# Scaling the rows before a transpose at the turns of blocks, in a two-layer diffusion trunk on one core

## Chip, cores and metric

The kernel runs on one core of a Trainium2 chip. The metric is the device time of one execution in microseconds (us). Five engines matter: TensorE (PE, matrix products, with its weight loads shown as PEld), VectorE (DVE), ScalarE (ACT), GpSimd (POOL) and SyncE (SP), whose queue starts the transfers.

## What is computed

The reference is one inference step of a trunk of two layers over 384 tokens (128 context tokens and 256 latent ones) of width 1024. Cut to the part that the change touches:

```
def rmsnorm(x, g):
    return x * lax.rsqrt(jnp.mean(x * x, axis=-1, keepdims=True) + EPS) * g

def trunk_layer(x, ...):
    h = rmsnorm(x, norm_mix_pre) * (1 + sc1) + sh1
    mix = mixer(h)                                   # retention | long convolution | mLSTM
    x1 = x + g1 * rmsnorm(mix, norm_mix_post)
    h = rmsnorm(x1, norm_ffn_pre) * (1 + sc2) + sh2
    return x1 + g2 * rmsnorm(conv_ffn(h), norm_ffn_post)   # up, conv and gate, down
```

## The kernel before

The tokens are three blocks `t` of 128: block 0 is the context, blocks 1 and 2 the latent tokens. Every large product is made from operands split in a high part (float32r) and a low part, the rest: `hh`, `hl` are the parts of the activations, `hi`, `lo` those of the weights, and a product is the sum hh·hi + hh·lo + hl·hi. The high part is a cast on ACT (`copy`, L281), the low part a subtraction on DVE (`tt`, L258). In traces a weight tile that comes from the first load of a stage is called `aside`.

A **turn** is a place where a block's rows become the operand of the next stage. For each block `t`:

- `residual` (L1382): two squares on ACT over the finished products (`junk<-b`), their mean on DVE (`rs`), the root on GpSimd (`rr`, L294), two products with the gate on DVE (`yg`), two updates of the rows `x` (L269).
- `norm_pre` (L776): two squares of the new rows on ACT (`junk<-x`), mean and root as above, then DVE scales the 128x128 identity by the root of each row, which gives a diagonal `diag`.
- `norm_P` (L792): for each half `c` of the width, four 128x128 products of the rows with that diagonal. Each puts 128 columns of the rows, scaled and transposed, into PSUM.
- `norm_M` (L800): the shift and scale of the modulation, four per half (`hf`): the left half on ACT, the right one on DVE (at the block turn both halves of block 1 on ACT). Two `hf` tiles rotate.
- `norm_S` (L813): the split of `hf` into `hh` (ACT) and `hl` (DVE).

There are three kinds of turn. At the start (`start`) the three blocks of the input are normed. At the **FFN turn** of each layer, `w_out` (L1417) finishes the blocks in the order 0, 1, 2; `norm_ffn` of block 0 goes before the last products of block 2, and `first_up` in `ffn` (L1457) norms block 1, multiplies the context tokens (128 of the 384) with the first pair of up weights `w` into the accumulators `a`, norms block 2, multiplies the context tokens with the second weights `w1` into `b`, then does the rest of `a` on the 256 latent tokens and of `b`. At the **block turn**, the end of layer 0, `ffn` runs the last two chunks of the down products, `down(14, [t])` and `down(15, [t])` (12 products each) for each block, norms block 0 within block 2's share, and `group("m", 1, 0)` (L828) norms blocks 1 and 2 and multiplies the three blocks with the first weights of layer 1's mixer.

The order on each engine is not written out by hand. The code issues instructions in the order of the program, some with a raised priority (`high_priority(offset=300)`) or tied behind another (`issue_after`), and a scheduler sets the order of each engine's instructions when the kernel is built. An engine then takes them in that order.

## Time and profile before

| | us |
|---|---|
| runs shown, median of 3 | 1334.61 (1334.31 to 1337.97) |
| profiled execution, its own time | 1334.32 |
| its span, first to last instruction | 1332.5 |
| PE busy | 1317.8 |
| DVE busy | 911.9 |
| ACT busy | 567.9 |
| GpSimd busy | 34.7 |

The profiled execution lasts 1.8 us longer than the span of its instructions and stands 0.3 us below the median of the runs. Matrix products are pipelined and the ends shown for them are modelled, so the distance from start to start is the time that a product takes of PE; its duration is longer. An idle stretch is put down to the instruction that released the engine last.

### The profile page before, as it was taken

How to read it: one execution, taken by the hardware profiler on the slowest of the kernel's cores; microseconds unless marked ns; L12 is line 12 of the kernel's file. 1: busy time of each engine (PE TensorE's matmuls, PEld its weight loads, DVE VectorE, ACT ScalarE, POOL GpSimd, SP SyncE). 2: the span in 40 equal slices, each digit the busy share in tenths (PEclk: the TensorE clock that was granted, in tenths of full speed). 3: DMA queues.
4: the chain of work that ended last, by engine and by line, in shares of the span. 5: the costliest groups of instructions: out<-in, count | busy, mean ns of one | idle time of the engine just before them, and what ended most of it. 6: DMA issues, size and time to landing. Idle time of an engine off the chain costs nothing.

```text
span 1332.5 us, 19422 instructions
## 1 busy us (share of the span) xinstructions
PE 1317.8 (99%) x7503; PEld 1202.0 (90%) x7503; DVE 911.9 (68%) x1634; ACT 567.9 (43%) x944; POOL 34.7 (3%) x64
## 2 busy tenths in 40 slices
PE   8999999999999999999999999999999999999998
PEld 2788899899999999989999999988999999999997
DVE  6647676578879889889566678756785545545445
ACT  3644353463333333333366544546433333333333
POOL 1100000000000000000000000000000000000000
PEclk9999999999999999999999999999999999999999
DMA  9884524524666666665445332433455333333331
GB/s 357 293 318 152 192 85 132 194 84 158 217 206 218 216 211 204 209 226 179 163 128 176 97 97 88 132 120 122 159 186 171 127 119 135 128 120 134 127 124 51
DMA packets 61437, 218.32 MB, mean 164 GB/s; under 512 B 7246, under 2 KB 9488, under 8 KB 58016
## 3 DMA queue, kind: packets, MB, share of 16 engines
q1 hardware_dynamic: 61344, 217.07, 47.7%
q8 instruction: 59, 0.97, 0.3%
q14 instruction: 34, 0.28, 0.1%
HBM read 211.11 MB, written 5.94 MB: 163 GB/s over the span
## 4 chain that ended last, share of the span: by engine, by line
PE 95%; DVE 2%; DMA 1%; issue 1%; ACT 1%; POOL 0%; DVEq 0%; POOLq 0%; ACTq 0%
PE b L211 93%; PE b L215 1%; DMA raw<-in_w_in_m 1%; DMA mraw<-in_w_mod 1%; DVE lo L258 0%; DVE x L269 0%; POOL rr L294 0%; DVE fw L258 0%; DVE mr L953 0%; ACT hi L281 0%; ACT junk L277 0%; ACT hf L277 0%; DVE modbm L269 0%; DVE yg L258 0%; DVE ev L258 0%
## 5 line engine op out<-in xcount | busy, mean ns | idle before, releaser
L258 DVE TENSOR_TENSOR lo<-raw,hi 128x1024 fp32r<-128x1024 f32 (+3 forms) x288 | 320.9, 1129 | 187.8 <-ACT hi L281 186.1
L281 ACT CAST hi<-raw 128x1024 fp32r<-128x1024 f32 (+3 forms) x288 | 275.2, 974 | 395.6 <-PE b L211 376.4
L211 PE MATMUL b<-hh,lo 128*128 128x384 f32 (+1 forms) x1120 | 367.3, 336 | 0.0
L211 PE MATMUL b<-hh,hi 128*128 128x384 f32 (+2 forms) x1120 | 364.3, 334 | 0.0
L211 PE MATMUL b<-hl,hi 128*128 128x384 f32 x1088 | 361.8, 337 | 0.0
L211 PEld LDWEIGHTS b<-hh,lo 128*128 128x128 f32 x1120 | 208.2, 188 | 0.1
L211 PEld LDWEIGHTS b<-hh,hi 128*128 128x128 f32 x1120 | 205.8, 188 | 2.2 <-issue 0.8
L211 PEld LDWEIGHTS b<-hl,hi 128*128 128x128 f32 x1088 | 203.8, 188 | 1.2
L269 DVE SCALAR_TENSOR_TENSOR cv<-b,pcol,cv 128x127 f32<-128x127 f32 (+1 forms) x256 | 100.6, 414 | 82.6 <-ACT cv L277 78.1
L211 PE MATMUL b<-hi,hh 128*128 128x384 f32 (+2 forms) x444 | 155.4, 353 | 0.0
L211 PE MATMUL b<-lo,hh 128*128 128x384 f32 (+2 forms) x450 | 154.5, 349 | 0.0
L211 PE MATMUL b<-hi,hl 128*128 128x384 f32 (+2 forms) x444 | 153.9, 350 | 0.0
L211 PE MATMUL b<-lo,gh 128*128 128x512 f32 x384 | 151.1, 393 | 0.0
L211 PE MATMUL b<-hi,gl 128*128 128x512 f32 x384 | 150.5, 392 | 0.0
L211 PE MATMUL b<-hi,gh 128*128 128x512 f32 x384 | 150.5, 392 | 0.0
L269 DVE SCALAR_TENSOR_TENSOR macc<-mraw,sil,macc 128x512 f32<-128x512 f32 x196 | 132.4, 745 | 0.0
L277 ACT ACTIVATE cv<-b,pcol 128x384 f32<-128x384 f32 x64 | 43.0, 672 | 176.2 <-PE b L211 176.0
L211 PEld LDWEIGHTS b<-hi,gh 128*128 128x128 f32 x384 | 72.1, 188 | 18.8 <-issue 4.2
L211 PEld LDWEIGHTS b<-hi,hh 128*128 128x128 f32 x444 | 83.3, 188 | 5.9 <-issue 2.2
L211 PEld LDWEIGHTS b<-hi,hl 128*128 128x128 f32 x444 | 83.4, 188 | 5.6 <-issue 2.4
L211 PEld LDWEIGHTS b<-lo,hh 128*128 128x128 f32 x450 | 84.6, 188 | 3.0 <-issue 0.2
L211 PEld LDWEIGHTS b<-hi,gl 128*128 128x128 f32 x384 | 72.1, 188 | 15.1
(251 smaller groups left out, 1247.1 us busy)
## 6 DMA issues: line engine op xcount, KB each, us to landing
raw<-in_w_up SPq DMA_DIRECT2D x128, 512.0 KB, 4.4
mraw<-in_w_mod SPq DMA_DIRECT2D x40, 1024.0 KB, 7.3
raw<-in_w_down SPq DMA_DIRECT2D x64, 512.0 KB, 4.1
raw<-in_w_in_r SPq DMA_DIRECT2D x32, 384.0 KB, 3.9
raw<-in_w_in_m SPq DMA_DIRECT2D x24, 384.0 KB, 4.6
raw<-in_w_out SPq DMA_DIRECT2D x16, 512.0 KB, 3.9
raw<-in_w_in_h SPq DMA_DIRECT2D x12, 512.0 KB, 3.7
mraw<-in_w_mod SPq DMA_DIRECT2D x8, 512.0 KB, 6.8
```

The costliest lines, as they stand in the source:

```text
L211: self.pe = self.nc.tensor.matmul(out, lhsT=lhsT, rhs=rhs, start=start, stop=stop, **kw)
L215: self.pe = self.nc.tensor.transpose(out, in_, self.ident[:n, :n])
L258: self.dve = self.nc.vector.tensor_tensor(o, a, b, op)
L269: self.dve = self.nc.vector.scalar_tensor_tensor(o, a, s, b, op0, op1)
L277: self.scalar = self.nc.scalar.activation(o, a, f, **kw)
L281: self.scalar = self.nc.scalar.copy(o, a)
```

## The change

Three edits:

- `norm_pre` can scale the rows themselves (`rows=True`): the left half on DVE, the right half on ACT, into two of four new tiles `xs` of 128x512. `norm_P` then transposes those tiles on PE instead of multiplying the rows with a diagonal. This is used for blocks 0 and 1 at each FFN turn and for all three blocks at the block turn; block 2 at the FFN turns and the start keep the diagonal.
- In `first_up` the context products of `b` take hh·hi and hl·hi ahead of the latent part of `a`, not hh·hi alone; afterwards `b` does these two for the latent tokens and hh·lo for all tokens.
- At the block turn the norm of block 0 stands behind block 2's first 12 down products, not ahead of them.

```diff
-    def norm_pre(self, t):
+    def norm_pre(self, t, rows=False):
...
         r = self.rms(s2)
+        self.scaled[t] = rows
+        if rows:
+            a, b = self.xn[t] = [self.tmp.tile([128, 512], F32, tag="xs", name=self.nm("xs"), bufs=4) for _ in range(2)]
+            self.ts(a, self.x[t][:, :512], r, ALU.mult)
+            self.act(b, self.x[t][:, 512:], AF.Copy, scale=r)
+            return
         d = self.tmp.tile([128, 128], F32, tag="diag", name=self.nm("diag"), bufs=3)
...
     def norm_P(self, t, c, ps):
         for k in range(4):
-            self.mm(ps[:, 128 * k:128 * k + 128], self.x[t][:, 512 * c + 128 * k:512 * c + 128 * k + 128], self.xn[t])
+            o = ps[:, 128 * k:128 * k + 128]
+            if self.scaled[t]:
+                self.tp(o, self.xn[t][c][:, 128 * k:128 * k + 128])
+            else:
+                self.mm(o, self.x[t][:, 512 * c + 128 * k:512 * c + 128 * k + 128], self.xn[t])
...
                     self.residual(t, self.accs[t], g)
-                    self.norm_pre(t)
+                    self.norm_pre(t, rows=t < 2)
...
-                up_part(b, w1, (0, 128), ((hh, 0), (hl, 0), (hh, 1)), product((0,), range(2), range(KD)))
+                up_part(b, w1, (0, 128), ((hh, 0), (hl, 0), (hh, 1)), product(range(2), range(2), range(KD)))
...
-                up_part(b, w1, (128, T), ((hh, 0),), product((0,), range(2), range(KD)), start=False)
-                up_part(b, w1, (0, T), (None, (hh, 1), (hl, 0)), product((1, 2), range(2), range(KD)))
+                up_part(b, w1, (128, T), ((hh, 0), (hl, 0)), product(range(2), range(2), range(KD)), start=False)
+                up_part(b, w1, (0, T), (None, None, (hh, 1)), product((2,), range(2), range(KD)))
...
             for t in range(NT):
+                down(14, [t])
                 if t == 2 and l + 1 < DEPTH:
                     self.norm_T_after(0, (l + 1, 0, 1, 0, 0), self.h1, lambda c: self.bank(6 + c))
-                down(14, [t])
                 down(15, [t])
...
-                        self.norm_pre(t)
+                        self.norm_pre(t, rows=True)
```

`tp` is `nc.tensor.transpose(out, in_, self.ident)`. At the block turn the first change reaches PE as follows. PE before, from the norm of block 1 (`diag_6497` times `x_2605`) into the mixer's first products; `b_1192`, `b_1193`, `b_1194` are the sums of blocks 0, 1 and 2, `aside` and `hi` the high weights of the first and second load:

```order
L211 MATMUL b_1201_6594<-diag_6497,x_2605 128x128 x4
L211 MATMUL b_1203_6606<-diag_6497,x_2605 128x128 x4
L211 MATMUL b_1192_6575<-aside_6399,hh_6369 128x400 x4
L211 MATMUL b_1192_6575<-hi_6582,hh_6369 128x400 x2
L211 MATMUL b_1192_6575<-hi_6584,hh_6369 128x400 x2
L211 MATMUL b_1192_6575<-aside_6399,hl_6370 128x400 x4
L211 MATMUL b_1192_6575<-hi_6582,hl_6370 128x400 x2
L211 MATMUL b_1192_6575<-hi_6584,hl_6370 128x400 x2
```

PE of the change at the same place; the sums of blocks 0 and 1 are `b_1197` and `b_1198`, and `hi_6608`, `hi_6610` are the two tiles of the second load:

```order
L215 MATMUL b_1206_6620<-c_ident,xs_6519 128x128 x4
L215 MATMUL b_1208_6632<-c_ident,xs_6520 128x128 x4
L211 MATMUL b_1197_6601<-aside_6419,hh_6389 128x400 x4
L211 MATMUL b_1197_6601<-hi_6608,hh_6389 128x400 x2
L211 MATMUL b_1198_6602<-aside_6419,hh_6389 128x400 x4
L211 MATMUL b_1197_6601<-hi_6610,hh_6389 128x400
L211 MATMUL b_1198_6602<-hi_6608,hh_6389 128x400 x2
L211 MATMUL b_1198_6602<-hi_6610,hh_6389 128x400
L211 MATMUL b_1197_6601<-hi_6610,hh_6389 128x400
L211 MATMUL b_1197_6601<-aside_6419,hl_6390 128x400 x4
L211 MATMUL b_1197_6601<-hi_6608,hl_6390 128x400 x2
```

Before, block 0 is multiplied through; now seven products of block 1 stand among the first products of block 0. ACT before, from the split of block 0's left half to the shift of block 1 (`raw_6578` and `raw_6580` are the second load of weights, cast in quarters of 400 columns):

```order
L281 CAST hh_6369<-hf_6504 128x4x128
L277 ACTIVATE junk_6491,s_1170_6488<-x_2605 128x512
L281 CAST hi_6582<-raw_6578 128x400 x2
L281 CAST hi_6584<-raw_6580 128x400
L281 CAST hh_6369<-hf_6516 128x4x128
L281 CAST hi_6584<-raw_6580 128x400
L277 ACTIVATE junk_6549,s_1180_6547<-b_647_3118 128x512
L277 ACTIVATE junk_6552,s_1180_6547<-b_648_3119 128x512
L277 ACTIVATE hf_6599<-b_1201_6594,modT_4639 128x128 x4
```

ACT of the change, from the split of block 0's left half (`hf_6540`) to the cast of the last quarter (`raw_6606`); `xs_6597` is the scaling of block 2:

```order
L281 CAST hh_6389<-hf_6540 128x4x128
L277 ACTIVATE junk_6576,s_1184_6571<-b_650_3139 128x512
L281 CAST hh_6389<-hf_6552 128x4x128
L277 ACTIVATE hf_6625<-b_1206_6620,modT_4659 128x128 x4
L277 ACTIVATE junk_6588,s_1190_6587<-x_2607 128x512
L281 CAST hh_6389<-hf_6625 128x4x128
L277 ACTIVATE junk_6590,s_1190_6587<-x_2607 128x512
L277 ACTIVATE hf_6637<-b_1208_6632,modT_4659 128x128 x2
L277 ACTIVATE xs_6597<-x_2607,rr_6594 128x512
L277 ACTIVATE hf_6637<-b_1208_6632,modT_4659 128x128 x2
L281 CAST hi_6610<-raw_6606 128x400
L281 CAST hh_6389<-hf_6637 128x4x128
```

The third and fourth quarters of the weights were cast ahead of the squares of block 2's products; now they stand behind the scaling of block 2's rows. At the FFN turn the third place is the second pair of up weights on PE. Before, behind the context products of `b` (`b_613`, `b_614` with `hi_2856`, `hi_2858`), the latent part of `a`, and then:

```order
L211 MATMUL b_613_2850<-hh_2589,hi_2856 128x256 x4
L211 MATMUL b_613_2850<-hh_2589,hi_2858 128x256 x4
L211 MATMUL b_614_2851<-hh_2589,hi_2856 128x256 x4
L211 MATMUL b_614_2851<-hh_2589,hi_2858 128x256 x4
L211 MATMUL b_613_2850<-hh_2589,lo_2857 128x384 x4
L211 MATMUL b_613_2850<-hh_2589,lo_2859 128x384 x4
L211 MATMUL b_614_2851<-hh_2589,lo_2857 128x384 x4
L211 MATMUL b_614_2851<-hh_2589,lo_2859 128x384 x4
L211 MATMUL b_613_2850<-hl_2590,hi_2856 128x384 x4
```

In the change the context products of `b`, now `b_615` and `b_616`, which stand behind the diagonal of block 2:

```order
L211 MATMUL b_627_2940<-diag_2847,x_2607 128x128 x4
L211 MATMUL b_629_2952<-diag_2847,x_2607 128x128 x4
L211 MATMUL b_615_2854<-hh_2589,hi_2860 128x128 x4
L211 MATMUL b_615_2854<-hh_2589,hi_2862 128x128 x4
L211 MATMUL b_616_2855<-hh_2589,hi_2860 128x128 x4
L211 MATMUL b_616_2855<-hh_2589,hi_2862 128x128 x4
L211 MATMUL b_615_2854<-hl_2590,hi_2860 128x128 x4
L211 MATMUL b_615_2854<-hl_2590,hi_2862 128x128 x4
L211 MATMUL b_616_2855<-hl_2590,hi_2860 128x128 x4
L211 MATMUL b_616_2855<-hl_2590,hi_2862 128x128 x4
L211 MATMUL b_613_2852<-hh_2589,aside_2664 128x256 x4
```

The 16 products hl·hi on 384 tokens have become 16 on 128 tokens here and 16 on 256 tokens behind the latent part of `a`.

## Rows read from the trace of the kernel before

**Rows 1.** The page, first part: an engine's busy time, share of the span, instructions.

```profile
PE 1317.8 (99%) x7503; PEld 1202.0 (90%) x7503; DVE 911.9 (68%) x1634; ACT 567.9 (43%) x944; POOL 34.7 (3%) x64
```

**Rows 2.** Waits of PE, whole span: us in total, times, longest.

```profile
PE b L211 <- DVE diag L263: 0.7, 3, 0.3
```

**Rows 3.** The chain that ended last, in order of time: start us, us, what.

```profile
279.50 201.47 PE b L211 x1134
```

**Rows 4.** Timeline of PE at the block turn: start us, us, line, operation, count.

```profile
691.07 1.95 PE L211 MATMUL b<-diag,x 128*128 128x128 f32 x16
...
698.37 1.95 PE L211 MATMUL b<-diag,x 128*128 128x128 f32 x16
...
700.07 0.98 PE L211 MATMUL b<-aside,hh 128*128 128x400 f32 x4
...
707.56 1.95 PE L211 MATMUL b<-diag,x 128*128 128x128 f32 x16
...
715.38 0.34 PE L211 MATMUL b<-hi,hh 128*128 128x384 f32 x1
```

**Rows 5.** Timeline of ACT and DVE at the block turn.

```profile
692.16 1.51 ACT L277 ACTIVATE hf<-b,modT 128x128 f32<-128x128 f32 x4 [0.20 <-PE b L211]
...
694.35 0.61 ACT L281 CAST hh<-hf 128x512 fp32r<-128x512 f32 x1
...
694.86 0.63 ACT L277 ACTIVATE junk<-x 128x512 bf16<-128x512 f32 x1
...
695.49 1.37 ACT L281 CAST hi<-raw 128x400 fp32r<-128x400 f32 x3
...
696.65 0.29 DVE L263 TENSOR_SCALAR diag<-c_ident,rr 128x128 f32<-128x128 f32 x1 [0.41 <-POOL rr L294]
...
697.29 0.52 ACT L281 CAST hi<-raw 128x400 fp32r<-128x400 f32 x1
...
704.66 0.29 DVE L263 TENSOR_SCALAR diag<-c_ident,rr 128x128 f32<-128x128 f32 x1 [0.73 <-POOL mpl L945]
```

**Rows 6.** Forms of the two products, ns min/median/max; one timeline and window row.

```profile
L211 PE MATMUL b<-diag,x x192: 270/275/377, 33.7 to 927.0; 128*128 128x128 f32 x192
...
L215 PE MATMUL b<-c_ident,hs x36: 270/272/322, 146.6 to 892.1; 128*128 128x128 f32 x36
...
733.54 1.47 PE L215 MATMUL b<-c_ident,k 128*96 128x128 f32 x12
...
733.50:735.00 1.50, 1.50 (x15) 1.46 (x13) 1.40 (x4) 1.26 (x3) 0.00 (x0) 1.00 0.61 229
```

**Rows 7.** Forms of the elementwise operations: ns min/median/max, over the span.

```profile
L263 DVE TENSOR_SCALAR macc<-mraw,sil x28: 478/482/489, 314.8 to 962.2; 128x512 f32<-128x512 f32 x28
...
L263 DVE TENSOR_SCALAR diag<-c_ident,rr x12: 278/286/291, 33.4 to 924.3; 128x128 f32<-128x128 f32 x12
...
L277 ACT ACTIVATE junk<-x x24: 617/630/634, 24.5 to 922.7; 128x512 bf16<-128x512 f32 x24
```

**Rows 8.** Timeline of PE at the first FFN turn.

```profile
274.49 2.05 PE L211 MATMUL b<-diag,x 128*128 128x128 f32 x16
...
279.50 2.05 PE L211 MATMUL b<-diag,x 128*128 128x128 f32 x16 [0.19 <-DVE diag L263]
...
288.46 1.98 PE L211 MATMUL b<-hh,hi 128*128 128x128 f32 x16
...
290.27 2.61 PE L211 MATMUL b<-hh,aside 128*128 128x256 f32 x20
...
296.05 2.05 PE L211 MATMUL b<-hh,hi 128*128 128x256 f32 x16
...
297.94 2.99 PE L211 MATMUL b<-hh,lo 128*128 128x384 f32 x16
...
300.76 2.99 PE L211 MATMUL b<-hl,hi 128*128 128x384 f32 x16
...
303.59 0.34 PE L211 MATMUL b<-hh,hi 128*128 128x384 f32 x1
```

More of the change, by code (lines that the diff above doesn't have):

```diff
@@ L416, in setup @@
         self.queue = []
-        self.xn = {}
+        self.xn, self.scaled = {}, {}
     def start(self, fp):
```

## The prediction

> **What bounds the kernel.** I read the page's busy times first: TensorE (PE) is busy for 1317.8 of 1332.5 us [rows 1], so time is won only by giving PE less to do, and lost whenever PE waits. The waits of PE say how little it waits: the largest entry that touches this change is 0.7 us, in three pieces, for the diagonal that VectorE (DVE) builds [rows 2]. The chain in order of time confirms it: behind the first FFN turn it runs on PE alone for 201 us [rows 3]. A microsecond that PE gains or loses at a turn is therefore kept up to the end. So each turn has to be laid out on PE, and beside it the two engines that feed it, ScalarE (ACT) and DVE, each of which takes its instructions in the order printed above.
>
> **What PE saves.** Before, a turn of one token block issues 8 products with the diagonal, which the trace counts as 16 passes; from the start of the second such batch at the block turn to the next product is 700.07 - 698.37 = 1.70 us [rows 4]. At the FFN turn 16 passes of the same width take 290.27 - 288.46 = 1.81 us [rows 8]. A transpose is one pass: 12 of them span 1.47 us of which the last has 0.27 to itself, so (1.47 - 0.27)/11 = 0.109 us each [rows 6], and 8 take 0.87. A turned block saves 0.83 to 0.94 us, I take 0.89. Seven blocks change (two at each FFN turn, three at the block turn): -6.2 us, if PE waits no longer than before.
>
> **What the split of the context products costs.** 16 products on 384 tokens become 16 on 128 and 16 on 256, in each layer. From the starts of such batches: 128 wide 1.81 us (288.46 to 290.27), 256 wide 1.89 (296.05 to 297.94), 384 wide 2.83 (300.76 to 303.59) [rows 8]. Narrow products hardly get cheaper, so this adds 1.81 + 1.89 - 2.83 = 0.87 us a layer, 1.7 us in all. It puts 1.8 us more of products under the third block's norm, but PE went from the 16 context products straight into the 256-wide ones there, at 290.27 [rows 8], so no wait is there to cover.
>
> **What the scaling costs.** A diagonal took 0.29 us on DVE. The left half of the rows takes about 0.48, the duration of the same operation on 128x512 [rows 7]. The right half on ACT is not in the trace. Its nearest row is the square of the same 512 columns, 0.63 [rows 7]; a 128x128 activation with a column as scale, 1.51/4 = 0.38, is the lower bound [rows 5], and I let it go up to 0.8, a quarter more than the square. I take 0.63. Seven of them are 4.4 us on ACT, which is far from full over the whole span, but at the turns it stands in the chain: squares, mean, root, scaling, transposes, shift, split, products. I laid out both turns step by step, every engine in its printed order, an instruction starting when its engine is free and its inputs are there, durations from the trace. For the order before, this gives 303.5 for the end of the FFN turn and 715.1 for that of the block turn, where the trace has 303.59 [rows 8] and 715.38 [rows 4]; so the layout holds to 0.3 us.
>
> **FFN turn, first layer.** The transposes of block 0 start 0.2 us later than the diagonal products did at 274.49 and still end 0.7 earlier. Those of block 1 find PE waiting 1.05 us for the scaled rows, since ACT has the scaling of block 0 and the first weight casts ahead of the squares of block 1; they start at 279.4, hardly before the 279.50 of the diagonal [rows 8]. Then the split of block 0, queued on ACT behind the second scaling, comes 0.8 us too late in two pieces. Of 1.8 us of saved work 0.25 is left, and the extra products take 0.87: **+0.6 us**. The second layer has the same orders: **+1.2 us** for both.
>
> **Block turn.** PE reaches block 2's middle, 12 products of 0.23 us after 691.07 [rows 4], at 693.8; there now stand the transposes of block 0, 2.7 us later than the diagonal products did. Their shift on ACT started at 692.16 [rows 5]; now it also stands behind the second square of block 1 (694.86 plus 0.73 with its sum [rows 5]), so at 695.6, and its last quarter behind the scaling of block 1, which waits for that block's root until 697.1 (the diagonal had it at 696.65 [rows 5]). The split of block 0, which came at 694.35 [rows 5], comes at 698.6 and 699.7, where PE wants it at 698.5: waits of 0.75 and 0.4. After only six products of block 0 PE's order now asks for block 1, whose split is ready at 702.9: a wait of 2.2. Then it asks for the third quarter of the high weights. That cast was done by 697.8 (rows at 695.49 and 697.29 [rows 5]); now it stands on ACT behind the scaling of block 2, whose root comes at 704.4 (before, the diagonal began at 704.66 [rows 5]), and two shifts, so it ends at 706.2: a wait of 2.6. Two more, 0.4 for the second half of block 1 and 0.6 for block 2, follow. With 0.2 for block 1's scaling before its transposes, that is 0.2 + 0.75 + 0.4 + 2.2 + 2.6 + 0.4 + 0.6 = 7.1 us of waits, against 0.2 in my layout of the order before, and 3 x 0.87 = 2.6 us of saved work: the turn ends at 719.4 in place of 715.1, **+4.3 us**. What follows (the load of the spectra waits for PE's last use of a tile in this turn) moves with it. The loads of the next weights wait for the late subtraction and move by 4 to 5 us as well; I cost that at nothing, 0.4 at most.
>
> **Sum.** 1.2 + 4.3 = **+5.5 us**. With the scaling on ACT at 0.45 it is 5.2, at 0.8 it is 6.8. Against the profiled execution's 1334.3 that is 1339.8; the median of the runs is 0.3 higher, so I forecast **1340.1 us**, 0.4% slower.
>
> One rule is to be weighed here. The rows show a transpose lasting 0.272 us, like a diagonal pass (0.275), but following each other at 0.109, at a granted clock of 1.00, in a stretch that is mostly transposes [rows 6]. The Trainium skill, TensorE: Matmul & The Clock Gate, Part 4 (PE-mode transpose), has a transpose at about 275 ns in a kernel's context and says that transposes do not count as busy for the clock. The duration agrees with that page; that each takes its place in the queue for so long the rows deny; by it the sum would be rival 3's.
>
> **Rivals.** (1) Faster: PE's saving stands and the waits do not end last, -6.2 + 1.7 = -4.5 us, 1330.1. For it speaks that PE hardly waits now [rows 2]. It decides if block 1's split at the block turn is ready when PE has done six products there, at 699.4, and the weight cast at 700.1; my layout has them 3.5 and 6 us too late. A chance of 0.06. (2) The waits are there but shorter: with every step on ACT, DVE and GpSimd a tenth shorter than the rows say (overlap between neighbours), the layout gives +3.0, so 1337.6; with 15% off, +1.1. Chance 0.18. (3) Transposes do not stream, each 0.27 us long: the layout then gives +1.4 at each FFN turn and +5.2 at the block turn, +8.0 and 1342.6. Against it, the 0.109 of [rows 6]. Chance 0.02; it is the mechanism of the rule above. (4) The change saves PE nothing, if a transpose of four-byte data should need the two passes of a product after all: 7 x 0.87 = 6.1 us more work, of which the waits hide all but the FFN turns' share, 2 x 0.9; +7.3 us, 1341.9. Against it, twelve transposes leave twelve records [rows 6]. Chance 0.02, on the slower side. The forecast itself has 0.72.
>
> **How the numbers follow.** A measurement of this kernel tells about 0.3%, 4.0 us, from no change: slower means above 1338.6. Of the forecast's 0.72 I put 0.65 above that line and 0.07 below; with rivals 3 and 4 slower has 0.69. Rival 2 and the 0.07 make no change 0.25. Faster is rival 1, 0.06. The range runs from +1.2 us (rival 2 with 15% off, 1335.8) to +7.4 (scaling at 0.8 and the late loads, 1342.0).
>
> **What would show it.** In the changed profile I expect the busy time of diagonal passes to fall from 192 to 80 records and 56 transposes more; PE's waits to name ACT's split tile and the cast of the raw weights at the block turn, together 5 us or more; the third quarter of the weights cast at about 705.7; and a PE start of the next products near 719.5. At the FFN turns the products should end 0.4 to 0.9 later than before. The prediction is wrong if PE's waits at the block turn stay under 2 us, or if block 1's split comes before 700.

## The result, and the profile after

The changed kernel takes 1348.2 us, median of 6 runs (1342.86 to 1351.05), against 1334.32 for the kernel before (1332.69 to 1337.97, 6 runs): 1.009 times as long, 95% interval 1.007 to 1.0109, some 14 us more. The forecast of 1340.1 had the sign and missed the size; its range ended at 1342.0. The profiled execution took 1350.06 us, its span is 1348.3 against 1332.5. The runs also differ in the mean clock that TensorE (PE) was granted, which the profiler gives for each: 0.989 to 0.996, and the three slowest runs have the three lowest clocks. Of 102 runs of the kernel before, beside the experiments below, all but 6 are at 0.997 or higher. Two single runs far off the rest, one of the kernel before (3506.52 us) and one of the kernel with the later diagonal (6084.48 us), are left out of every figure.

The page's first part, the line that answers to [rows 1] (busy time, share, instructions):

```profile
PE 1326.2 (98%) x7479; PEld 1207.7 (90%) x7479; DVE 912.7 (68%) x1634; ACT 571.8 (42%) x951; POOL 35.1 (3%) x64
```

PE is busy for longer, although its instructions got fewer. The waits of PE over the whole span (us in total, times, longest), the lines that answer to [rows 2]:

```profile
PE b L211 <- ACT hh L281: 3.3, 5, 1.9
PE b L215 <- DVE xs L263: 2.9, 5, 1.2
...
PE b L211 <- ACT hi L281: 1.8, 1, 1.8
```

These are the waits that the forecast named: block parts that ScalarE (ACT) splits too late, scaled rows that are late, and one late cast of weights. The forms of the products with the diagonal and of the transposes (duration in ns: least, median, most), which answer to [rows 6]:

```profile
L211 PE MATMUL b<-diag,x x80: 275/275/522, 33.9 to 939.4; 128*128 128x128 f32 x80
...
L215 PE MATMUL b<-c_ident,xs x56: 272/273/329, 273.9 to 931.4; 128*128 128x128 f32 x56
```

192 records became 80, and 56 transposes came, as forecast. Where the time went is seen in PE's timeline. The first FFN turn (start us, us, engine, line, operation, how many, idle time before it and who ended it), which answers to [rows 8]:

```profile
273.27 0.40 PE L211 MATMUL b<-hi,hl 128*128 128x512 f32 x1
...
278.87 1.09 PE L215 MATMUL b<-c_ident,xs 128*128 128x128 f32 x8 [1.16 <-DVE xs L263]
...
280.71 2.41 PE L211 MATMUL b<-hh,aside 128*128 128x128 f32 x11 [0.23 <-ACT hh L281]
282.92 3.62 PE L211 MATMUL b<-hl,aside 128*128 128x128 f32 x16
286.33 1.05 PE L211 MATMUL b<-hh,aside 128*128 128x128 f32 x4
...
309.75 0.34 PE L211 MATMUL b<-hh,hi 128*128 128x384 f32 x1
```

The second layer has the same turn, with the same order and nearly the same waits:

```profile
924.99 0.40 PE L211 MATMUL b<-hi,hl 128*128 128x512 f32 x1
...
930.59 1.09 PE L215 MATMUL b<-c_ident,xs 128*128 128x128 f32 x8 [1.16 <-DVE xs L263]
...
932.43 1.44 PE L211 MATMUL b<-hh,aside 128*128 128x128 f32 x11 [0.23 <-ACT hh L281]
933.71 0.61 PE L211 MATMUL b<-hl,aside 128*128 128x128 f32 x4
934.54 1.55 PE L211 MATMUL b<-hl,aside 128*128 128x128 f32 x12 [0.22 <-DVE hl L258]
935.93 0.61 PE L211 MATMUL b<-hh,aside 128*128 128x128 f32 x4
...
955.40 0.34 PE L211 MATMUL b<-hh,hi 128*128 128x384 f32 x1
```

Compare 16 products of the `hl` part: from 282.92 to the next batch at 286.33 they take 3.41 us in the first turn; in the second, 4 of them at 933.71 and 12 at 934.54 take 2.22 with the wait of 0.22. In the kernel before, the same turns begin behind the products at 274.10 and 912.64, and the second ends at 942.12:

```profile
274.10 0.40 PE L211 MATMUL b<-hi,hl 128*128 128x512 f32 x1
...
912.64 0.40 PE L211 MATMUL b<-hi,hl 128*128 128x512 f32 x1
...
942.12 0.34 PE L211 MATMUL b<-hh,hi 128*128 128x384 f32 x1
```

From the last product ahead of block 0's turn to the first product of the next up pass the kernel before needs 29.49 us in the first layer (274.10 to 303.59, its end in [rows 8]) and 29.48 in the second; the changed kernel needs 36.48 (273.27 to 309.75) and 30.41 (924.99 to 955.40). So the turn itself costs **0.93 us**, and in the first layer something added 6.1. Stretches of 10 us, with PE's busy time and, third number from the end, the granted clock, show what:

```profile
280.00:290.00 10.00, 9.77 (x49) 9.62 (x48) 6.23 (x15) 5.75 (x15) 1.10 (x2) 0.55 0.16 52
...
700.00:710.00 10.00, 7.20 (x33) 5.14 (x31) 8.72 (x20) 9.55 (x27) 1.54 (x3) 0.88 0.55 184
710.00:720.00 10.00, 8.20 (x30) 7.69 (x30) 2.19 (x4) 2.78 (x6) 1.13 (x6) 0.61 0.25 71
...
930.00:940.00 10.00, 8.95 (x77) 8.67 (x77) 8.14 (x18) 8.53 (x22) 1.11 (x3) 1.00 0.16 54
```

and the first of them in the kernel before:

```profile
280.00:290.00 10.00, 10.00 (x92) 10.00 (x92) 8.14 (x19) 7.46 (x19) 1.10 (x2) 1.00 0.05 18
```

In the first FFN turn, behind the two waits, PE ran at half its clock (0.50, 1.2 GHz in place of 2.4) from 281.0 to 294.6, and at the block turn from 707.6, inside the wait of 1.90 us shown next, to 717.9. At the second FFN turn, and in the same places before, the clock is 1.00. The block turn on PE, which answers to [rows 4], from the last down product of block 1:

```profile
696.23 0.39 PE L211 MATMUL b<-hi,gl 128*128 128x512 f32 x1
...
703.23 1.09 PE L215 MATMUL b<-c_ident,xs 128*128 128x128 f32 x8 [0.23 <-DVE xs L263]
704.89 1.00 PE L211 MATMUL b<-aside,hh 128*128 128x400 f32 x4 [0.57 <-ACT hh L281]
...
708.52 1.70 PE L211 MATMUL b<-aside,hh 128*128 128x400 f32 x4 [1.90 <-ACT hh L281]
712.02 2.22 PE L211 MATMUL b<-hi,hh 128*128 128x400 f32 x5 [1.80 <-ACT hi L281]
...
727.63 0.34 PE L211 MATMUL b<-hi,hh 128*128 128x384 f32 x1
```

and on ACT, which answers to [rows 5]:

```profile
707.87 0.60 ACT L281 CAST hh<-hf 128x512 fp32r<-128x512 f32 x1
...
710.14 0.72 ACT L277 ACTIVATE xs<-x,rr 128x512 f32<-128x512 f32 x1 [0.16 <-POOL mpl L955]
...
711.45 0.52 ACT L281 CAST hi<-raw 128x400 fp32r<-128x400 f32 x1
```

ACT turns to block 1's high part at 707.87, and the cast of the third quarter of the weights stands behind the scaling of block 2 (710.14), at 711.45; PE waits for both. Counted from the same product, block 1's last down product (the turn of block 0 now stands 12 products, 2.75 us, later), the block turn takes 31.40 us (696.23 to 727.63). Before, that product was

```profile
690.84 0.39 PE L211 MATMUL b<-hi,gl 128*128 128x512 f32 x1
```

and the turn took 24.54 us, to 715.38 [rows 4]: **+6.9 us**.

A third loss has nothing to do with waits. One pair of up products, 96 products of 128x384, in the middle of layer 1 of the kernel before, from its first product to the first down product behind it:

```profile
1043.96 0.34 PE L211 MATMUL b<-hh,hi 128*128 128x384 f32 x1
...
1060.61 0.39 PE L211 MATMUL b<-hi,gh 128*128 128x512 f32 x1
```

and in the changed kernel:

```profile
1056.47 0.34 PE L211 MATMUL b<-hh,hi 128*128 128x384 f32 x1
...
1073.43 0.39 PE L211 MATMUL b<-hi,gh 128*128 128x512 f32 x1
```

16.65 us became 16.96, with the granted clock at 1.00 in both. Each profile shows pairs of 16.64 and of 16.96 us and a few others. In layer 1 of the kernel before two of 14 pairs are slow and one is between, 0.8 us lost; in the changed kernel 12 are slow, 3.8 us. **+3.0 us**. In the profiled execution 7.0 + 6.9 + 0.9 + 3.0 = 17.8 us; the up pairs of layer 0 and the stretch ahead of the first turn gave 1.8 back, and PE's last product comes 16.0 us later than before.

### The profile page after: what moved, and what is told of

It reads as the page before. It is cut to its first block, busy times and chain, and to the rows that moved or that the text cites. A ratio compares the mean times of both kernels' runs of the same rounds, so it can differ in the third digit from the quotient of the medians.

```text
span 1348.3 us, 19364 instructions
## 1 busy us (share of the span) xinstructions
PE 1326.2 (98%) x7479; PEld 1207.7 (90%) x7479; DVE 912.7 (68%) x1634; ACT 571.8 (42%) x951; POOL 35.1 (3%) x64
## 4 chain that ended last, share of the span: by engine, by line
PE 92%; DVE 4%; DMA 2%; ACT 1%; issue 1%; POOL 0%; SPq 0%; DVEq 0%; POOLq 0%; ACTq 0%
PE b L211 90%; DMA mraw<-in_w_mod 1%; PE b L215 1%; DVE lo L258 1%; DVE x L269 1%; POOL rr L294 0%; ACT junk L277 0%; ACT hf L277 0%; DVE macc L269 0%; DMA w<-in_f_w 0%; DVE fw L258 0%; ACT hi L281 0%; DVE yg L258 0%; DVE mr L963 0%; ACT xs L277 0%
## 5 line engine op out<-in xcount | busy, mean ns | idle before, releaser
L211 PE MATMUL b<-hl,hi 128*128 128x384 f32 (+2 forms) x1120 | 364.3, 334 | 0.0
```

What stands on the lines that cost most here:

```text
L211: self.pe = self.nc.tensor.matmul(out, lhsT=lhsT, rhs=rhs, start=start, stop=stop, **kw)
```

## The experiments

Each was measured beside runs of the kernel before; ratios are to those runs. "Turn" is the time from the product ahead of block 0's turn to the next stage, as above; the clocks of the turns come from one profiled execution of each kernel, the mean clocks from all its runs. The diffs are cut to the lines that matter, and the remarks behind # are not in the code.

**The change in pieces: FFN turns alone, block turn alone.** Scaled rows and the new context order, without the block turn's:

```diff
-                        self.norm_pre(t, rows=True)      # block turn
+                        self.norm_pre(t)
...
-                down(14, [t])
                 if t == 2 and l + 1 < DEPTH:
                     self.norm_T_after(0, ...)
+                down(14, [t])
```

> Scaled rows and the new order of the context products at the two FFN turns alone; the block turn as in the kernel before (diagonal products, block 0 ahead of block 2's down products). Theory C: the waits of 1.2 us at the FFN turns are there, the clock falls behind them in some executions: 0.9 us a turn without a fall, 7 with one, so single runs from 1336 to 1348 us and a median near 1342. Theory W (the terms of the forecast at full clock): two turns at 0.9, 1336.2 us, little scatter.

1342.58 us, ratio 1.0065 (1.0035 to 1.0096). The five runs lie at 1338.0, 1338.2, 1342.6, 1344.1 and 1348.2 us, with mean clocks of 0.999, 0.999, 0.996, 0.994 and 0.990: the same kernel is 10 us slower where its clock was lower. In the profile the first turn takes 35.30 us, at half clock behind it, the second 30.41. And the reverse, with the FFN turns and the context order of the kernel before:

```diff
-                    self.norm_pre(t, rows=t < 2)         # FFN turn
+                    self.norm_pre(t)
...
-                up_part(b, w1, (0, T), (None, None, (hh, 1)), product((2,), ...))
+                up_part(b, w1, (0, T), (None, (hh, 1), (hl, 0)), product((1, 2), ...))
```

> Scaled rows and the later place of block 0 at the block turn alone; the FFN turns as in the kernel before. Theory C: 4.3 us of waits as in the forecast and about 2.6 us for 10 to 12 us at a lower granted clock behind them, 1339 to 1342 us. Theory W: 1338.6 us with clock 1.00 throughout.

1339.73 us, 1.0046 (1.003 to 1.0062), all five runs between 0.994 and 0.995. In the profile the clock is at half from 701.6 to 708.6, at the block turn and, but for the start and the end of the program, nowhere else; the even means suggest that it falls there every time. The turn is 6.6 us longer than before.

**Fill the wait at the FFN turn.** Six products into the wait for block 1's scaled rows, in the changed kernel:

```diff
+                    for _ in range(6):
+                        self.mm(a[0], w[0][0][:, :128], w[0][0][:, 256:256 + T])
                 self.norm_ffn(l, 1)
```

> The change, with six further products of 128x384 (0.17 us each, 1.04 us in all, into the bank that the next products overwrite) put on TensorE where it waits 1.16 us for block 1's scaled rows at each FFN turn; the result is the same, the transposes stay. If the idle time at the turn is what lets the granted clock fall (theory C): granted clock 1.00 behind the first FFN turn, both FFN turns cost about 0.9 us over the kernel before instead of 7.0 and 0.9, the block turn stays as it is, and the median falls from 1348.2 to about 1342 us, with less scatter. If the transposes, which stay, bring the clock down (theory T), or if the cost is not the clock's at all (theory W): the clock row and the time stay, 1347 to 1350 us.

1349.85 us, 1.0117 (1.0091 to 1.0143). The wait is gone and the clock falls all the same, later. PE's timeline, and two stretches of 2 us (the granted clock is again third from the end):

```profile
279.57 1.09 PE L215 MATMUL b<-c_ident,xs 128*128 128x128 f32 x8
...
281.40 1.55 PE L211 MATMUL b<-hh,aside 128*128 128x128 f32 x12 [0.34 <-ACT hh L281]
...
284.00:286.00 2.00, 2.00 (x14) 2.00 (x13) 1.75 (x6) 1.88 (x5) 0.49 (x1) 0.62 0.00 0
286.00:288.00 2.00, 2.00 (x11) 2.00 (x11) 1.22 (x3) 0.62 (x1) 0.06 (x1) 0.50 0.00 0
```

Theory C in its plain form, that the long wait brings the fall, does not hold.

**A wait without transposes.** In the kernel before:

```diff
+        for _ in range(late):                            # late = 2 for block 1 of an FFN turn
+            self.ts(o, self.x[t][:, :512], r, ALU.mult)  # o is not used
         self.ts(d, self.ident, r, ALU.mult)
```

> The kernel before, with block 1's diagonal matrix at each FFN turn made about 1 us later by two unused VectorE scalings of 128x512 (0.48 us each) ahead of it; no transposes, the result is the same. Theory C: TensorE waits 1.0 to 1.4 us there and nothing else changes, so the granted clock falls behind the turn in some executions: single runs from 1336.5 to 1348 us. Theory T (the transposes bring the fall): 1.1 us a turn and no more, 1336.5 us, clock 1.00 behind both turns.

1336.13 us, 1.0018 (1.0005 to 1.0031), nine runs with clocks of 0.997 to 0.999, both turns 30.60 us. PE waits longer at this place than in the changed kernel, and nothing falls:

```profile
280.52 2.05 PE L211 MATMUL b<-diag,x 128*128 128x128 f32 x16 [1.30 <-DVE diag L263]
```

With four such operations (`late = 4`) the order that came out also put part of block 0's products ahead of block 1's turn:

> The kernel before with four unused VectorE scalings ahead of block 1's diagonal matrix instead of two: by the 1.30 us that two gave (0.56 us each) TensorE waits about 2.4 us at each FFN turn, as much as waits and transposes of block 1 together in the changed kernel; no transposes. C and T alike say that enough idle time brings the fall: in some executions 6 us behind a turn, so single runs of 1339 (4.4 us of waits) up to 1350 us. If it never falls (theory N: the transposes matter in another way than as idle time), 1338.5 to 1339 us in every run, clock 0.997 or higher.

1340.79 us, 1.0045 (1.0033 to 1.0057). The wait stands ahead of block 0's products now, with a second one behind five of them, and the clock falls, without any transpose:

```profile
281.65 0.77 PE L211 MATMUL b<-hh,aside 128*128 128x128 f32 x5 [1.16 <-ACT hh L281]
282.75 1.00 PE L211 MATMUL b<-hh,aside 128*128 128x128 f32 x4 [0.32 <-ACT hh L281]
...
283.00:284.00 1.00, 0.97 (x5) 0.78 (x5) 1.00 (x5) 0.00 (x0) 0.06 (x1) 0.50 0.00 0
```

The last line is a stretch of 1 us, at a granted clock of 0.50. Both turns take 32.8 us.

**Ordinary products in place of block 1's transposes**, in the kernel with the FFN turns alone:

```diff
+            if self.scaled[t] and t == 1:
+                self.mm(o, self.xn[t][c][:, 128 * k:128 * k + 128], self.ident)
+            elif self.scaled[t]:
-            if self.scaled[t]:
                 self.tp(o, self.xn[t][c][:, 128 * k:128 * k + 128])
```

> As the kernel with the change at the FFN turns alone, but block 1's scaled rows are turned by ordinary fp32 products with the identity (two passes, 16 records) instead of 8 transposes; the wait of 1.16 us for those rows stays, block 0 keeps its transposes. After the first four runs theory C (idle time alone) has lost ground: 1.30 us of idle time at a turn without transposes brought no fall, and with the wait filled the clock still fell. Theory T now: a stretch of transposes counts for the clock like idle time, and the two add up. T: with block 1 on ordinary products only the wait and the earlier transposes are left, the clock falls rarely or never, runs at 0.998 or 0.999; a turn costs about 0.9 + 0.9 - 0.2 = 1.6 us over the kernel before, so 1338 us with little scatter (1342.6 median, up to 1348 with the transposes). C: granted clocks between 0.990 and 0.999 as with the change at the FFN turns alone, median over 1341 us.

1338.41 us, 1.0031 (1.0019 to 1.0043), clocks 0.996 to 0.999, turns 30.48 and 30.50 us at a clock of 1.00. This looked like a proof of theory T. But the slower products also gave ACT 0.9 us more, and the two small waits among block 0's products had gone with the transposes. So T was tried by itself.

**Transposes without any wait, and products in their place**, in the kernel before:

```diff
                 self.norm_ffn(l, 1)
+                    for _ in range(24):                       # tp24
+                        self.tp(a[0][:, :128], self.x[0][:, :128])
+                    for _ in range(12):                       # mm12, two passes each
+                        self.mm(a[0][:, :128], self.x[0][:, :128], self.ident)
```

> The kernel before with 24 useless transposes (fp32, 128x128, about 0.106 us each, 2.5 us) at each FFN turn, right behind the diagonal products of block 1, into a bank that the next products overwrite; TensorE has no wait there. Theory T (transposes count for the clock like idle time): the granted clock falls behind the turn in most executions although TensorE is never idle; 5.1 us of transposes plus 1.5 to 6 us a turn, single runs from 1341 to 1352 us, clocks from 0.990 to 0.997. Theory C (idle time alone): 1340 us in every run, clock 0.998, as with 12 ordinary products in their place.

> The same with 12 ordinary fp32 products of the same 128x128 blocks with the identity (two passes each, 24 passes at about 0.111 us, 2.7 us) in place of the 24 transposes. T and C alike: no fall, 5.3 us more than the kernel before, 1340 us, clock as in the kernel before. A fall here would say that any added work at this place brings one, and that neither theory holds.

1338.73 us, 1.0034 (1.0023 to 1.0046), and 1338.31, 1.0032 (1.0019 to 1.0045): the same. Clocks 0.997 to 0.999 with the transposes, turns 32.10 us both times, and what follows 24 transposes runs at full speed:

```profile
280.04 2.78 PE L215 MATMUL b<-c_ident,x 128*128 128x128 f32 x24
282.58 1.98 PE L211 MATMUL b<-hh,aside 128*128 128x128 f32 x16
```

2.5 us of transposes by themselves bring no fall, so theory T does not hold in the form that was tried. That transposes add to a wait or a gap is not ruled out: with the wait filled, 16 of them and a gap of 0.34 us were followed by a fall.

**Close the gaps, or make only a gap.** In the kernel with the FFN turns alone four products behind block 1's transposes; and in the kernel before an unused pass of ACT ahead of block 0's second high part:

```diff
                 self.norm_ffn(l, 1)
+                    for _ in range(4):                        # fill_gap
+                        self.mm(a[0], w[0][0][:, :128], w[0][0][:, 256:256 + T])
...
+            self.act(jk, hf.rearrange("p k n -> p (k n)"), AF.Square)   # gap_only: t == 0, c == 1
             self.copy(hh[:, ks, tok], hf)
```

> The kernel with the change at the FFN turns alone, with four further products of 128x384 (0.70 us) right behind block 1's transposes, so that the high and low parts of block 0 are there when their products come: the two gaps of 0.23 us among those 128-column products go, the wait of 1.16 us ahead of the transposes stays, and so do all transposes. Twenty-four transposes without idle time brought no fall, so theory T is out. Theory G: what tips the clock is a gap inside the row of short products behind the turn (each profile with a fall at an FFN turn had one: 0.23 and 0.23, 0.34, or 0.32 us), not the wait ahead of them (1.30, 1.16 and 0.97 us brought none). G: no fall, every run at 0.997 or higher, 1338 to 1340 us, under the 1342.6 us without the added products. Theory C' (idle time and transposes of the turn together, however they lie): falls as in the change at the FFN turns alone, median over 1341 us, single runs up to 1348 us.

> The kernel before, with one unused ScalarE pass of 128x512 ahead of the cast of block 0's second high half at each FFN turn, so that TensorE waits 0.4 to 0.9 us inside the row of block 0's 128-column products; no transposes, and no other wait than the 0.19 us for block 1's diagonal matrix. Theory G: the clock falls behind it in a part of the executions, single runs from 1335.5 up to 1345 us, granted clocks down to 0.993. Theory C' (the sum of idle time and transposes decides, which is under 1.1 us here, less than the 1.49 us that brought no fall in the kernel with the later diagonal matrix): no fall, 1335.5 to 1336.5 us in every run, 0.997 or higher.

With the gaps closed 1338.19 us, 1.0028 (1.0017 to 1.004). All 12 runs are at 0.997 to 0.999, and one alone is above 1340.4 (1343.8, at 0.997). Three of five were at 0.996 or lower without the four products (measured on another chip, which may play a part). The long wait and all the transposes are still there, and the turns take 30.41 and 30.40 us:

```profile
278.53 1.09 PE L215 MATMUL b<-c_ident,xs 128*128 128x128 f32 x8 [1.16 <-DVE xs L263]
...
280.17 1.90 PE L211 MATMUL b<-hh,aside 128*128 128x128 f32 x16
```

But a gap alone does not bring the fall either: 1335.36 us, 1.0008 (0.9998 to 1.0018), one of 12 runs at 0.996, the rest at 0.997 or higher, both turns 30.07 us, with the gap where it was wanted:

```profile
281.82 1.45 PE L211 MATMUL b<-hh,aside 128*128 128x128 f32 x11 [0.38 <-ACT hh L281]
```

Theory G is half right. The four products also put 0.7 us of wide products ahead of the short ones, and whether that or the closed gaps held the clock was not separated. In a table, from the profile of each kernel:

| kernel | wait ahead, us | transposes | gaps among block 0's products, us | turns, us | clock behind |
|---|---|---|---|---|---|
| before | 0.19 | none | none | 29.49, 29.48 | 1.00 |
| gap only | 0.19 | none | 0.38 | 30.07, 30.07 | 1.00 |
| later diagonal | 1.30 | none | none | 30.60, 30.60 | 1.00 |
| block 1 by products | 1.16 | 8 | none | 30.48, 30.50 | 1.00 |
| gaps closed | 1.16 | 16 | none | 30.41, 30.40 | 1.00 |
| 24 transposes | 0.19 | 24 | none | 32.10, 32.10 | 1.00 |
| four late operations | 1.16 | none | 0.32 | 32.77, 32.78 | 0.50 behind both |
| wait filled | none | 16 | 0.34 | 33.68, 30.43 | 0.50 behind the first |
| FFN turns alone | 1.16 | 16 | 0.23, 0.23 | 35.30, 30.41 | 0.50 behind the first |
| the change | 1.16 | 16 | 0.23, then 0.22 in the second | 36.48, 30.41 | 0.50 behind the first |

Every profile with a fall at an FFN turn has a gap among block 0's products and a wait or transposes close ahead of it (with four late operations the wait is ACT's, for block 0's high part); neither of the two alone brought one in a profile. Both together do not always: three kernels have the same waits in the second layer and no fall there.

**Block 0 alone by scaled rows at the FFN turns**, the rest of the kernel before:

> The kernel before with scaled rows and transposes for block 0 alone at the FFN turns: no wait of 1.16 us, 8 transposes less work for TensorE at each turn (0.89 us a turn); blocks 1 and 2, the order of the products and the block turn as before. Waits: 0.2 us longer for block 0, and the split of block 0 is not later than what waits for it. T and C: no fall, 1333 us (0.7 us a turn saved). If 0.85 us of transposes alone are enough for a fall, single runs up to 1345 us.

```diff
-                    self.norm_pre(t)
+                    self.norm_pre(t, rows=t == 0)
```

1335.48 us, 1.0004 (0.9995 to 1.0014): nothing gained, where 1333 was expected. The turns take 29.49 and 29.51 us as before; PE arrives 0.8 us earlier at block 1, and its wait for that diagonal grows from 0.19 to 0.96 us:

```profile
277.70 2.05 PE L211 MATMUL b<-diag,x 128*128 128x128 f32 x16 [0.96 <-DVE diag L263]
```

**The new order of the context products alone, and what sets the pace.** First the order by itself, in the kernel before (the second half of the diff for the block turn alone, reversed):

> The kernel before with the new order of the context products alone (16 products of 384 columns become 16 of 128 and 16 of 256); no scaled rows. By the starts in the trace after (16 of 128 columns in 1.78 us, 16 of 256 in 1.88, 16 of 384 in 2.83) 0.83 us a layer, so +1.7 us, 1335.8 us, clock as in the kernel before. A rival that the new order is what brings the clock down (products of 128 columns in a long row) would show runs from 1336 to 1348 us.

1337.97 us, 1.0026 (1.0017 to 1.0035), clock as before. The second turn takes 30.27 in place of 29.48 us, +0.8; the rest is the pace of layer 1's up products, 3.8 us lost in place of 0.8. Then 16 small products, without and with the new order:

```diff
+                for _ in range(16 if p == 2 else 0):
+                    self.mm(ab[0][:, :16], wu[0][0][:, :128], hh[0][:, :16])
                 self.channel_major(ab, wu, hh, hl)
```

> The kernel before, with 16 small products (16 columns each) of no use ahead of the second pair of up products in each layer, overwritten by what follows; the order of the context products is that of the kernel before. In all traces so far a pair of up products (96 products of 128x384) runs in 16.96 or in 16.64 us, and which pairs are slow goes with the 16 products that the new order of the context products adds: layer 1 loses 0.8 us over its 14 pairs without them and 3.8 us with them. Theory P (the count of products issued before them sets the pace): the pairs of layer 1 are slow and fast as in the changed kernel, 3.8 us, so 3.0 us more, beside 16 small products a layer at 0.03 to 0.11 us each: 1338.5 to 1341 us. Theory O (the order at the turn sets it, or what is stored where): 0.8 us as before, 1335.5 to 1338 us.

> The kernel with the new order of the context products alone (1338.0 us, 3.8 us lost to the pace of layer 1's up products), with the same 16 small products ahead of the second pair in each layer. Theory P: 32 products more than the kernel before; if the pace has two states that 16 products exchange, it is back at 0.8 us, and the time is 1336 to 1338.5 us, at or under that of the new order alone although work was added; if it has more states, something between 0.8 and 3.8. Theory O: the pace stays at 3.8 us, 1339 to 1341.5 us.

1338.98 us, 1.0032 (1.002 to 1.0044), and 1344.17, 1.0069 (1.0056 to 1.0082). The small products took more than I allowed, 1.96 us a layer, but the pace did not change: 0.8 us lost in layer 1 without the new order, 3.8 with it. Theory P falls. Last, the order without the cut:

```diff
-                up_part(b, w1, (0, T), (None, (hh, 1), (hl, 0)), product((1, 2), ...))
+                up_part(b, w1, (0, T), (None, (hl, 0), (hh, 1)), product((1, 2), ...))
```

> The kernel before, where b's last two passes of 384 columns are exchanged: the low-part activations first, the low-part weights last, as in the changed kernel, but no pass is cut in two and no product is added. The pace of the up products (0.8 us lost in layer 1 without the new order of context products, 3.8 with it; 16 added products did not change it). Theory O1 (which pass stands last ahead of the up products sets it): 3.8 us in layer 1, and nothing else changes, so 1337.5 to 1338.5 us. Theory O2 (the cutting of the pass sets it): 0.8 us, and the time of the kernel before, 1334 to 1335.5 us.

1335.32 us, 1.0003 (0.9992 to 1.0013), 0.8 us lost in layer 1. So neither 16 products more nor the order of the last passes brings the slow pace. All seven profiles with the cut show it in layer 1 (3.8 us), and none of the thirteen without it. What is left is the cut itself or the new place of its first part; these two were not separated.

**The block turn's late casts.** In the kernel with the block turn alone, the casts of the second weight chunk moved ahead:

```diff
+            with self.tc.high_priority(offset=400) if l else nullcontext():
-            ws = [self.weights(key, l, c, ...) for c in range(2)]
+                ws = [self.weights(key, l, c, ...) for c in range(2)]
```

> The kernel with the change at the block turn alone (1339.7 us, block turn 6.6 us longer than before), with the four casts of the next stage's second weight chunk moved ahead of the scaling and the split on ScalarE. Two of them ran at the end of that queue (at 702.92 and 703.85 us), and TensorE waited 2.32 us for the first. Theory A (what costs at the block turn is ScalarE's queue, the casts last in it): that wait goes, the wait of 2.08 us for block 1's high part stays or shrinks by the products that can now run ahead, the clock falls for a shorter time or not at all; block turn 2 to 4 us longer than before, 1335.5 to 1337.5 us. Rival (the later place of block 0 and the scaled rows themselves): the wait only moves to the high parts, 1339 to 1340.5 us.

1336.87 us, 1.0018 (1.0009 to 1.0027), against 1339.73 without. PE's longest waits were, in the kernel with the block turn alone:

```profile
700.16 1.00 PE L211 MATMUL b<-aside,hh 128*128 128x400 f32 x4 [2.08 <-ACT hh L281]
703.48 2.22 PE L211 MATMUL b<-hi,hh 128*128 128x400 f32 x5 [2.32 <-ACT hi L281]
```

With the four casts ahead of the scaling of block 1 on ACT

```profile
693.37 1.81 ACT L281 CAST hi<-raw 128x400 fp32r<-128x400 f32 x4 [0.88 <-PE b L211]
```

the wait for the cast is gone. Left are 1.27 us for block 0's high part, 0.66 for block 1's scaled rows, two of 0.26 and 0.36 and, for block 1's high part,

```profile
707.80 1.00 PE L211 MATMUL b<-hi,hh 128*128 128x400 f32 x4 [1.24 <-ACT hh L281]
```

The clock stays at 1.00 up to the end of the turn, which is 2.0 us longer than before in place of 6.6. Theory A holds. The other part, block 0's place:

```diff
-                down(14, [t])
                 if t == 2 and l + 1 < DEPTH:
                     self.norm_T_after(0, ...)
+                down(14, [t])
```

> The kernel with the change at the block turn alone, but block 0 is turned ahead of block 2's first 12 down products, as in the kernel before. Theory A: the place gives block 0's split a head start of 2.75 us, so the wait of 0.57 us for it goes, but scalings, splits and casts still stand in one queue on ScalarE and the long waits (2.08 and 2.32 us) stay: 1338.5 to 1339.5 us (1339.7 with the later place). Rival (the later place is what costs): the block turn is within 1.5 us of the kernel before, 1335 to 1336 us.

1341.46 us, 1.0049 (1.0036 to 1.0061): above what either theory gave, and not faster than with the later place. The turn is 5.3 us longer than before; the waits moved together into one of 1.80 and one of 3.24 us for ACT's high parts. Most of the cost is there without the later place.

**The change without its dear parts:** block 1 by the diagonal at the FFN turns, the context order of before, the casts ahead.

> The change without the three parts found dear: block 1 keeps its diagonal products at the FFN turns, the context products keep the order of the kernel before, and at the block turn the casts of the next stage's second chunk stand ahead of the scaling. What is left of the change: scaled rows for block 0 at the FFN turns (1335.5 against 1334.7 us) and for all blocks at the block turn (1336.9 against 1335.1 us). If the parts add up: 1336 to 1337.5 us, clock 0.997 or higher, no fall at the turns, layer 1's pace 0.8 us; that is 11 to 12 us under the change as it stands, and 1.5 to 2.5 over the kernel before. If something of the change's cost has not been found, it shows here as a time over 1339 us.

1336.54 us, 1.0019 (1.0008 to 1.0029), FFN turns 29.50 us both, block turn 2.0 us longer than before, all at a clock of 1.00. The parts add up. From the medians: what is left of the change 1.8 us; late casts 5.6 (block turn alone) - 2.5 (casts ahead) = 3.1; the context order 3.3; block 1's scaled rows at the FFN turns 8.4 (FFN turns alone) - 3.3 - 0.8 (block 0 alone) = 4.3; together 12.5 of the 13.9 us. The intervals of the ratios leave each of these figures uncertain by 1 us or more, that of the FFN turns alone by 4, so the rest of 1.4 us is within them. No version found beats the kernel before.

## Why the prediction was wrong, and where it was right

**Right: the order of events.** The layout put the third quarter's cast at 705.7, to end at 706.2; block 1's last down product comes 5.4 us later in the profiled execution (696.23 against 690.84), so it was due at 711.1, and stands at 711.45. Block 1's split was to be ready at 702.9, so 708.3; PE goes on at 708.52. At the FFN turn 0.2 and 1.05 us and 0.8 in two pieces were forecast; the second layer has 0.19, 1.16 and 0.23 + 0.22. The waits that name ACT's split and the late cast at the block turn were to be 5 us or more together and are 4.6 (0.57 + 1.90 + 0.35 + 1.80). The split of the context products, 0.87 us by [rows 8], measured 0.8. The scaling on ACT takes 0.72 us, between the 0.63 taken and the 0.8 allowed. The passes saved on PE were there as computed; why they do not win at an FFN turn, as rival 1 would have it, the run with block 0 alone shows: even where no split is late, the wait for the next diagonal takes the whole gain back. Two bounds of the prediction are off by a little: 6.8 and 0.4 for the late loads make +7.2, not +7.4, and rival 2 with 15% off stands as +1.1 in one place and as +1.2 in another.

**Wrong: the sum at a clock of 1.00.** This is the step that failed most. Every duration came from rows at full clock, and the sum, "1.2 + 4.3 = +5.5 us", let each wait cost its own length. In the profiled execution the first FFN turn, at half clock behind its waits, took 6.1 us more than the second, and the block turn had 10 us at half clock: +6.9 us in place of +4.3, although half speed shortened its second long wait (1.80 us in place of 2.6; the four products ahead took 1.70 us in place of 1.00). From 712.02, the end of that wait, to 717.9 PE was busy at half clock, 5.9 us that would be some 2.9 at full clock (an estimate); without them the turn costs about 4.0. With two FFN turns at the 0.93 us measured at full clock the forecast's own terms come to 5.9 us against 5.5: the waits were laid out rightly, and what was left out is what they do to the clock, 6.1 + 2.9 us in this execution.

**Wrong: "What the split of the context products costs".** The step priced 16 narrow and 16 wider products where they stand and took everything behind for unmoved. The pace of layer 1's up products, hundreds of microseconds long, went from 0.8 to 3.8 us lost with the cut, so the term of 1.7 us was 1.6 + 3.0: the price on the spot was right, and the effect behind it had been put at nothing.

**The weighed rule.** The Trainium skill, TensorE: Matmul & The Clock Gate, Part 4 (PE-mode transpose), says that a transpose does not count as PE-busy in the same way, so that full clock does not engage. The run with 24 transposes of fp32 and no wait does not bear it out: clock 1.00 behind both turns, and the same time as with 12 products. It does not settle the rule either, since no run here leaves PE idle for 2.5 us in place of the transposes, and a wait of 1.30 us was not followed by a fall. Rival 3 is out: the 24 took 2.54 us (280.04 to 282.58), 0.106 each. So is rival 4: the 56 transposes left 56 records. The clock that the rule speaks of was the right question, and the forecast asked it of transposes alone and not of the waits.

**Open.** What exactly makes the clock fall at an FFN turn was not settled: a wait or transposes and then a gap among short products brought it in some executions, each alone in none or hardly any. Nor is a wait at a turn the only place for it. Six of the 20 profiles have about 3.4 us at half clock in layer 1's mixer, some 15 us behind the block turn, among them two kernels that change nothing near it (block 0 alone; the last passes exchanged, shown here), and the kernel before has none there:

```profile
732.00:734.00 2.00, 2.00 (x8) 2.00 (x8) 1.50 (x5) 0.77 (x2) 0.00 (x0) 0.54 0.00 0
```

So a run's mean clock of 0.996 or 0.997 does not by itself say that the clock fell at a turn. Nor is it known why a cut pass changes the pace of products that stand far behind it.

## What to carry to other kernels

On a kernel that TensorE bounds, a wait of a microsecond costs its own length only while the clock holds: where a change puts two or three small waits close together, read the granted clock behind them, in several executions, before trusting a sum. When work is taken off TensorE, look first at what the next block waits for: at the FFN turn here the producer was just in time, and the saved passes of block 0 became a wait. And order by hand what stands on a shared feeding engine ahead of the critical operations: moving four casts gave back about 3 us at a turn where three transposed blocks could save 2.7.

## What the runs showed of the hardware that was not expected

TensorE was granted half its clock behind 1.4 us of waits in two pieces, and kept it for 13.6 us although it was busy without a break; the same instructions in the next layer ran at full clock. 24 fp32 transposes in a row, 2.5 us, were not followed by a lower one. Products of 128x384 on one engine at the same clock ran in two steady paces, 16.64 or 16.96 us for 96, for hundreds of microseconds, and the pace was the same in layer 1 of each kernel with the same products at its turn. The scaling of 128x512 on ACT takes 0.72 us, where the square of the same columns takes 0.63.
